# Experts' results weighted as they leave PSUM and summed by an adding scatter

## The chip, the cores and the metric

One core of a Trainium2 chip runs one program for the whole model: TensorE (PE) multiplies matrices, VectorE (DVE), ScalarE (ACT) and GpSimd (POOL) do the rest, SyncE (SP) issues most of the loads and stores, and 16 DMA engines move the data. The metric is the time of one execution on the device in microseconds, lower is better. All data are 32-bit.

## The reference

The model has two layers over 1024 tokens of width 1024 and 256 context tokens. Layer 0 mixes with differential attention, layer 1 with windowed attention. After each mixer stands a mixture of experts: a router picks one of 4 groups and in it 2 of 8 experts, so each token goes to 2 of 32 experts. The context tokens go through the experts in layer 0 alone, so layer 0 sends 1280 tokens and layer 1 sends 1024. Cut to what matters here:

```
weights = (gate_g * jax.nn.softmax(top_v, axis=-1)).reshape(-1)
expert = (g[:, None] * EXPERTS_PER_GROUP + top_i).reshape(-1)
...
hidden = jax.nn.silu(x_blk @ w_gate[e]) * (x_blk @ w_up[e])
return hidden @ w_down[e]
...
out = jnp.zeros((n_tok + 1, d), t.dtype).at[buf_tok].add(yb * buf_w[:, None].astype(yb.dtype))
```

The sum of a token's two weighted results is multiplied by a gate row and added to the residual stream. After layer 1 the sum is normalised and written out.

## The kernel before, in words

Tokens are handled in tiles of 128: ten in layer 0 (`NT`; tiles 8 and 9 are the context), eight in layer 1 (`NX`). A matrix is multiplied in two parts, a rounded one and the remainder, so every weight chunk is first split by ScalarE (`ehi`, L1154) and VectorE (`elo`, L1156).

The experts (`moe`, L1161) run in the order of a list. An expert has six weight chunks of 1 MB, four for gate and up, two for down. They come through a ring of 12 slots filled by SP's queue (`ring_load`, L1123); from chunk 160 of 192 on, only 7 slots are left. SP issues a load when the slot's last reader is done. GpSimd gathers an expert's token rows (`gather`, L1177) two experts ahead by the list `tI`. The down products stand in one PSUM tile `y`; `result` (L1225) copies its two halves to SBUF, and `scatter` (L1182) writes its rows to `ybs` in DRAM, one row for each pair of token and choice, at the places in `dI` (twice the token plus the choice). An expert has up to 128 rows; places beyond the count point outside the table, and nothing is moved for them. A loop for experts with more than 128 rows (`overflow`, L1332) follows.

The order of the experts' work on PE, ACT, DVE and POOL is written out by hand (`manual_schedule`). Elsewhere a scheduler sets the order of instructions on each queue when the program is built, SP's queue always.

Layer 1 begins with the first layer's sums: per tile two loads of 512 KB (`load_y`, L1394), one for each choice, then `combine` (L1412): ScalarE multiplies the first result by its weight, VectorE multiplies the second and adds, the gate row multiplies on VectorE or GpSimd, VectorE adds to the residual. `norm1_a` and `norm1_b` follow, and the attention's products.

The end (`final`, L1421) loads sixteen tiles, builds diagonal matrices of the weights (`dg`), and lets TensorE mix the two results of tiles 1 to 7 (`mix`, L1451); VectorE multiplies by the gate row (L1452), adds (L1457) and normalises (L1464).

## Time and profile before

| | |
|---|---|
| runs timed alone | 2995.53 us median of 3 (2992.17 to 2997.57) |
| profiled execution | 2986.94 us, span 2985.0 us |
| granted TensorE clock, mean | 0.97 |
| PE / DVE / ACT / POOL busy | 93% / 78% / 73% / 30% of the span |
| DMA | 746 MB, 250 GB/s over the span |

A row of a timeline gives start, length, engine, line, operation and what is written from what, and in brackets the idle time before it with what ended it. A row of stretches gives the busy time of each engine in the stretch, the granted clock as a share of full speed, the mean busy share of the 16 DMA engines (transfers that overlap can take it over 1) and the GB/s moved. A row of lines gives count, total busy time, mean length and idle time before. Times of one execution are compared with that execution alone; busy shares over the whole span mix stages with different limits, so the stage is looked at first.

### The profile page before, as it was taken

What the parts mean: (1) busy time and instruction counts of PE and PEld (TensorE: products, weight loads), DVE (VectorE), ACT (ScalarE), POOL (GpSimd) and SP (SyncE); (2) the same over time, 40 slices, a digit from 0 to 9 for tenths busy, and PEclk for the clock granted to TensorE, in tenths of its full rate; (3) what the DMA queues carried; (4) which work ended last, traced back from release to release, by engine and by line L of the source; (5) the groups of instructions that cost most, each with busy time, mean ns of one, the idle gap of its engine ahead of it and who ended that gap; (6) DMA issues with size and microseconds to landing.
All of it is one profiled execution on the core that took longest, in us unless ns stands there. A gap on an engine that the chain in (4) does not pass through costs nothing. (4 is left out here: it accounts for less than half of the span.)

```text
span 2985.0 us, 44431 instructions
## 1 busy us (share of the span) xinstructions
PE 2786.2 (93%) x15263; PEld 2357.7 (79%) x15263; DVE 2340.4 (78%) x4063; ACT 2165.9 (73%) x3972; POOL 896.6 (30%) x839
## 2 busy tenths in 40 slices
PE   7999999999979979999999589998999799999996
PEld 4888888889868868888888478887888688888883
DVE  5778777777777779899998786665766799999987
ACT  5777777777678568888888578876553488888883
POOL 5756665665500011111110344655100111111110
PEclk9999999999989989999999699999999899999998
DMA  7644554454343689999999745444226799999996
GB/s 269 228 166 165 174 184 154 164 175 150 121 156 124 213 304 379 385 384 384 381 359 351 287 159 196 162 150 156 94 102 209 256 365 377 378 380 373 348 378 256
DMA packets 303502, 746.04 MB, mean 250 GB/s; under 512 B 24644, under 2 KB 80552, under 8 KB 287912
## 3 DMA queue, kind: packets, MB, share of 16 engines
q1 hardware_dynamic: 265320, 681.25, 63.4%
q0 software_dynamic: 19584, 41.98, 3.6%
q10 hardware_dynamic: 18368, 19.93, 1.9%
q8 instruction: 122, 2.00, 0.3%
q14 instruction: 108, 0.88, 0.1%
HBM read 681.13 MB, written 91.29 MB: 259 GB/s over the span
## 5 line engine op out<-in xcount | busy, mean ns | idle before, releaser
L1156 DVE TENSOR_TENSOR elo<-wr,ehi 128x1024 fp32r<-128x1024 f32 x768 | 894.4, 1219 | 106.3 <-ACT ehi L1154 106.3
L1154 ACT ACTIVATE ehi<-wr 128x1024 fp32r<-128x1024 f32 x768 | 765.7, 1065 | 6.7 <-DVE wts L1018 3.4
L344 PE MATMUL qkv<-w_hi,hT 128*128 128x384 f32 (+1 forms) x1920 | 542.0, 350 | 11.6 <-ACT hT L315 3.6
L344 PEld LDWEIGHTS qkv<-w_hi,hT 128*128 128x128 f32 x1920 | 351.2, 195 | 27.0 <-issue 10.8
L1183 POOL DMA_INDIRECT y_s<-yb,dI x64 | 65.6, 1025 | 966.8 <-ACT yb L1232 938.0
L344 PE MATMUL qkv<-w_lo,hT 128*128 128x384 f32 (+1 forms) x960 | 333.3, 347 | 0.0
L1222 PE MATMUL y<-ehi,hidT 128*128 128x512 f32 x1024 | 317.2, 391 | 2.4 <-ACT yb L1232 2.4
L1208 PE MATMUL pg<-ehi,xT 128*128 128x512 f32 x1024 | 291.9, 407 | 0.0
L1208 PE MATMUL pu<-ehi,xT 128*128 128x512 f32 x1024 | 281.9, 397 | 0.0
L605 DVE TENSOR_SCALAR_CACHE_REDUCE E<-S 128x1280 f32<-128x1280 f32 (+1 forms) x160 | 203.5, 1272 | 58.5 <-PE S L622 55.5
L1222 PEld LDWEIGHTS y<-ehi,hidT 128*128 128x128 f32 x1024 | 191.7, 188 | 44.0 <-ACT yb L1232 3.2
L613 ACT ACTIVATE E<-E,mx 128x1280 f32<-128x1280 f32 (+1 forms) x160 | 190.9, 1193 | 48.1 <-DVE E L605 46.9
L1208 PEld LDWEIGHTS pu<-ehi,xT 128*128 128x128 f32 x1024 | 187.9, 188 | 36.8
L1208 PEld LDWEIGHTS pg<-ehi,xT 128*128 128x128 f32 x1024 | 184.6, 190 | 33.5 <-ACT xT L1193 0.5
L864 PE MATMUL qkv<-woh,oT 128*128 128x512 f32 x576 | 200.2, 408 | 0.5 <-ACT oT L851 0.5
L1222 PE MATMUL y<-elo,hidT 128*128 128x512 f32 x512 | 199.4, 389 | 0.0
L344 PEld LDWEIGHTS qkv<-w_lo,hT 128*128 128x128 f32 x960 | 186.4, 194 | 6.2 <-issue 4.3
L620 PE MATMUL S<-K,Qh 128*128 128x512 f32 (+1 forms) x416 | 153.7, 370 | 17.7 <-DVE E L605 17.6
L227 ACT ACTIVATE mpr<-mraw,sf 128x256 f32<-128x256 f32 x320 | 145.3, 504 | 26.9 <-POOL macc L230 22.2
L1208 PE MATMUL pg<-elo,xT 128*128 128x512 f32 x512 | 159.0, 392 | 0.0
L1232 ACT ACTIVATE yb<-y 128x512 f32<-128x512 f32 x126 | 68.6, 595 | 124.4 <-PE y L1222 124.4
L1208 PE MATMUL pu<-elo,xT 128*128 128x512 f32 x512 | 158.2, 390 | 0.0
(306 smaller groups left out, 6482.7 us busy)
## 6 DMA issues: line engine op xcount, KB each, us to landing
wr<-in_wg SPq DMA_DIRECT2D x128, 1024.0 KB
wr<-in_wu SPq DMA_DIRECT2D x128, 1024.0 KB
wr<-in_wd SPq DMA_DIRECT2D x128, 1024.0 KB
hT<-hTs SPq DMA_DIRECT2D x100, 1024.0 KB
mraw<-in_mod_w SPq DMA_DIRECT2D x80, 512.0 KB
hTs<-hT SPq DMA_DIRECT2D x20, 1024.0 KB
c_y<-y_s SPq DMA_DIRECT2D x36, 512.0 KB
w_raw<-in_a_qkv SPq DMA_DIRECT2D x32, 384.0 KB
```

The source lines that it names most:

```text
L227: nc.scalar.activation(pr[v][:, q], raw[:, q], AF.Copy, scale=self.sf[:, 4 * i + q, v:v + 1])
L344: self.nc.tensor.matmul(ps[:, 0:n], hT[:, a, k, :], W[b][:, k, c0:c0 + n], start=(i == 0), stop=(i == 3 * KC - 1))
L605: nc.vector.tensor_scalar(E[:, 0:n], Sf[:, 0:n], -0.125, None, op0=OP.mult, op1=OP.min, accum_out=mx)
L613: nc.scalar.activation(E[:, 0:n], E[:, 0:n], AF.Exp, bias=mx, scale=-1.0, accum_out=acc)
L620: nc.tensor.matmul(Sf[:, n0:n0 + w], Qh[:, m, j * P:(j + 1) * P], K[h][:, m, o:o + w], start=True, stop=False)
L864: nc.tensor.matmul(y, oT[:, a, k, :], w[:, k, half * 512:half * 512 + 512], start=(i == 0), stop=(i == 3 * KC - 1))
L1154: nc.scalar.activation(hi, raw, AF.Copy)
L1156: nc.vector.tensor_tensor(lo[:, 0:c], raw[:, 0:c], hi[:, 0:c].bitcast(F32), op=OP.subtract)
L1183: nc.gpsimd.indirect_dma_start(out=self.ybs[l], out_offset=bass.IndirectOffsetOnAxis(ap=idx, axis=0), in_=yb, in_offset=None, bounds_check ...
L1208: nc.tensor.matmul(o, xt[:, a, k, :], w[:, q * 512:(q + 1) * 512], start=(k == 0 and a == 0 and w is hi), stop=(k == KC - 1 and w is lo))
L1222: nc.tensor.matmul(y[:, half, :], hT[:, a, k, :], w[:, f], start=(k == 0 and a == 0 and w is hi), stop=(k == 3 and w is lo))
L1232: nc.scalar.activation(yb[:, f], y[:, half, :], AF.Copy)
```

## The change

The table `ybs` has one row per token instead of two. Its rows are set to zero by 18 stores of a small zero tile, issued in the loop of attention 0. The router's weights are also written to DRAM (`ws`), two per token. For each expert GpSimd sets a column `we` to zero and gathers into it the 128 weights of the expert's rows, by `dI`. `result` multiplies by this column as it copies from PSUM. `scatter` goes by `tI` and has `compute_op=OP.add`: the DMA adds to the row that lies there. A tile's sum is then one load of 512 KB; `combine` multiplies by the gate row and adds, and `final` has neither the diagonals nor the mixing matmuls.

```diff
@@ consts
-        self.ybs = [dr.tile([2 * (NT, NX)[l] * P, D], F32, name=f"y_s{l}") for l in range(2)]
+
+        self.ybs = [dr.tile([(NT, NX)[l] * P, D], F32, name=f"y_s{l}") for l in range(2)]
+        self.ws = [dr.tile([2 * (NT, NX)[l] * P, 1], F32, name=f"w_s{l}") for l in range(2)]
+        self.zero = c.tile([P, 128], F32, name="zero")
+        nc.vector.memset(self.zero, 0.0)
@@ attention0, in the loop over heads and tiles
+                zeros = [self.ybs[l][t * P:(t + 1) * P, :] for l in range(2) for t in range((NT, NX)[l])][10 * (h - 1):10 * h] if h else []
                 for u, j in enumerate(range(NT) if nxt else ORDER0):
+                    for z in zeros[u:u + 1]:
+                        nc.sync.dma_start(z.rearrange("p (a b) -> p a b", a=8), bc(self.zero, 8, 1))
@@ finish, the last step of the router
             nc.vector.tensor_tensor(self.wts[:, 0:T, 1], gr, er, op=OP.mult)
+            nc.sync.dma_start(self.ws[l].rearrange("(t p a) o -> p t (a o)", p=P, a=2), self.wts[:, 0:T, :])
@@ moe
+            def gather_w(idx):
+
+                w = pl.tile([P, 1], F32, name="we", bufs=4)
+                nc.gpsimd.memset(w, 0.0)
+                nc.gpsimd.indirect_dma_start(out=w, out_offset=None, in_=self.ws[l],
+                                             in_offset=bass.IndirectOffsetOnAxis(ap=idx, axis=0),
+                                             bounds_check=2 * T * P - 1, oob_is_err=False)
+                return w
+
             def scatter(yb, idx):
+
                 nc.gpsimd.indirect_dma_start(out=self.ybs[l], out_offset=bass.IndirectOffsetOnAxis(ap=idx, axis=0),
-                                             in_=yb, in_offset=None, bounds_check=2 * T * P - 1, oob_is_err=False)
+                                             in_=yb, in_offset=None, bounds_check=T * P - 1, oob_is_err=False,
+                                             compute_op=OP.add)
...
-            def result(y, last=False):
+            def result(y, w, last=False):
...
-                        nc.vector.tensor_copy(yb[:, f], y[:, half, :])
+                        nc.vector.tensor_scalar(yb[:, f], y[:, half, :], w, None, op0=OP.mult)
...
-                        nc.scalar.activation(yb[:, f], y[:, half, :], AF.Copy)
+                        nc.scalar.activation(yb[:, f], y[:, half, :], AF.Copy, scale=w)
...
-                    yb = result(ys.pop(e), e == NE - 1)
-                    at(m + DSCAT, scatter, yb, self.dI[:, e:e + 1])
+                    yb = result(ys.pop(e), we.pop(e), e == NE - 1)
+                    at(m + DSCAT, scatter, yb, self.tI[:, e:e + 1])
...
                             ps[e] = [ps_g.tile([P, 512], F32, name=x) for x in ("pg", "pu")]
+                            we[e] = gather_w(self.dI[:, e:e + 1])
@@ load_y, combine
-    def load_y(self, l, t, pl, n=3, queues=None):
-        nc = self.nc
-        yt = [pl.tile([P, D], F32, name=f"c_y{a}", tag="c_y", bufs=2 * n) for a in range(2)]
-        for a in range(2):
-            (queues or (nc.sync, nc.sync))[a].dma_start(
-                yt[a], self.ybs[l][2 * t * P:2 * (t + 1) * P, :].rearrange("(p a) d -> p a d", a=2)[:, a, :])
+    def load_y(self, l, t, pl, n=3):
+        yt = pl.tile([P, D], F32, name="c_y", bufs=n)
+        self.nc.sync.dma_start(yt, self.ybs[l][t * P:(t + 1) * P, :])
         return yt
...
-        return self.load_y(l, t, pl, n), self.load_x(l, t, pl, CXB)
...
-        nc.scalar.activation(yt[0], yt[0], AF.Copy, scale=self.wts[:, t, 0:1])
-        nc.vector.scalar_tensor_tensor(yt[0], yt[1], self.wts[:, t, 1:2], yt[0],
-                                       op0=OP.mult, op1=OP.add)
-        eng.tensor_tensor(yt[0], yt[0], g2, op=OP.mult)
-        return lambda: nc.vector.tensor_tensor(xt, xt, yt[0], op=OP.add)
+        return self.load_y(l, t, pl, n + 1), self.load_x(l, t, pl, CXB)
+
+    def combine(self, yt, xt, g2, eng):
+
+        eng.tensor_tensor(yt, yt, g2, op=OP.mult)
+        return lambda: self.nc.vector.tensor_tensor(xt, xt, yt, op=OP.add)
@@ final
-            for t in range(1, NX):
-                dg[t] = pl.tile([P, 2, P], F32, name="dg", bufs=NX - 1)
...
-            def mix(t):
...
-                            nc.tensor.matmul(p[:, half, :], dg[t][:, a], y[t][a][:, f], start=(a == 0), stop=(a == 1))
-                    nc.vector.tensor_tensor(y0, p.rearrange("p a b -> p (a b)"), g2, op=OP.mult)
...
+            def add(t):
+
+                nc.vector.tensor_tensor(y[t], y[t], g2, op=OP.mult)
+                nc.vector.tensor_tensor(x[t], x[t], y[t], op=OP.add)
```

The order of instructions that the two programs hold shows where the new instructions stand. The first place is GpSimd's queue in the experts of layer 0, from the gather for expert 4 on; before (`xg` are gathered token rows, `h_s` the tokens, `y_s` the table of results, `yb` a result in SBUF):

```order
L1178 DMA xg_12188<-h_s_93,tI 128x1024
L1183 DMA y_s_98<-yb,dI 2560x1024
L1178 DMA xg_12186<-h_s_93,tI 128x1024
L1183 DMA y_s_98<-yb,dI 2560x1024
L1178 DMA xg_12187<-h_s_93,tI 128x1024
L1183 DMA y_s_98<-yb,dI 2560x1024
```

and after:

```order
L1186 DMA xg_12211<-h_s_93,tI 128x1024
L1201 DMA y_s_98<-yb,tI 1280x1024
L1193 MEMSET we 128x1
L1194 DMA we<-w_s_100,dI 128x1
L1186 DMA xg_12209<-h_s_93,tI 128x1024
L1201 DMA y_s_98<-yb,tI 1280x1024
L1193 MEMSET we 128x1
L1194 DMA we<-w_s_100,dI 128x1
L1186 DMA xg_12210<-h_s_93,tI 128x1024
L1201 DMA y_s_98<-yb,tI 1280x1024
```

For each expert a zeroing and a gather of the weight column came in ahead of the gather of rows; the scatter goes by `tI` into a table of half as many rows.

The second place is SP's queue early in attention 0, while the tiles of the first head are projected (`hTs` and `hT` are normalised tiles stored and loaded, `w_raw` and `mraw` weights); before:

```order
L317 DMA hTs_89<-hT 128x2048
L317 DMA hTs_90<-hT 128x2048
L487 DMA hT<-hTs_82 128x2048
L317 DMA hTs_91<-hT 128x2048
L487 DMA hT<-hTs_83 128x2048
L215 DMA mraw<-in_mod_w 128x4x256 x2
L330 DMA w_raw<-in_a_qkv 128x768
L487 DMA hT<-hTs_84 128x2048
```

and after:

```order
L321 DMA hTs_88<-hT 128x2048
L334 DMA w_raw<-in_a_qkv 128x768 x2
L321 DMA hTs_89<-hT 128x2048
L663 DMA y_s_98<-zero 1024x1x128 x2
L321 DMA hTs_90<-hT 128x2048
L491 DMA hT<-hTs_82 128x2048
L321 DMA hTs_91<-hT 128x2048
L663 DMA y_s_98<-zero 1024x1x128 x2
L491 DMA hT<-hTs_83 128x2048
L219 DMA mraw<-in_mod_w 128x4x256 x2
L491 DMA hT<-hTs_84 128x2048
L334 DMA w_raw<-in_a_qkv 128x768
```

Some of the 18 zero stores now stand between the stores and loads of tiles, one to three at a time.

The third place is SP's queue at the start of layer 1 (`c_y` results, `g` gate rows, `c_x` residual); before:

```order
L1398 DMA c_y_17986<-y_s_98 128x1024
L1398 DMA c_y_17987<-y_s_98 128x1024
L734 DMA g_1_17990<-mod_s_100 128x1024
L1398 DMA c_y_17992<-y_s_98 128x1024
L1398 DMA c_y_17993<-y_s_98 128x1024
L1398 DMA c_y_17996<-y_s_98 128x1024
L1398 DMA c_y_17997<-y_s_98 128x1024
L734 DMA g_0_18000<-mod_s_100 128x1024
L378 DMA cos<-in_cos 128x512
```

and after:

```order
L1416 DMA c_y<-y_s_98 128x1024
L741 DMA g_1_18176<-mod_s_104 128x1024
L1416 DMA c_y<-y_s_98 128x1024 x2
L741 DMA g_0_18182<-mod_s_104 128x1024
L382 DMA cos<-in_cos 128x512
L383 DMA sin<-in_sin 128x512
L741 DMA sink<-in_b_sink 128x16
```

One load stands for two, and the gate rows and the rope tables move up behind fewer loads.

## Rows read from the trace of the kernel before

**Rows 1.** The page, parts 1 and 2: PE's total, then 40 slices in tenths.
```profile
PE 2786.2 (93%) x15263; PEld 2357.7 (79%) x15263; DVE 2340.4 (78%) x4063; ACT 2165.9 (73%) x3972; POOL 896.6 (30%) x839
...
PE   7999999999979979999999589998999799999996
...
DVE  5778777777777779899998786665766799999987
...
PEclk9999999999989989999999699999999899999998
DMA  7644554454343689999999745444226799999996
```

**Rows 2.** Stretches of 100 us in layer 0's and layer 1's experts.
```profile
core 0: us, PE busy (x) PEld busy (x) DVE busy (x) ACT busy (x) POOL busy (x), PEclk, DMA share, GB/s
...
1300.00:1400.00 100.00, 100.00 (x474) 82.55 (x473) 89.83 (x89) 82.36 (x101) 15.11 (x12) 1.00 1.02 386
...
2500.00:2600.00 100.00, 100.00 (x474) 82.51 (x473) 91.52 (x93) 83.51 (x103) 13.64 (x11) 1.00 1.02 377
```

**Rows 3.** Timeline: layer 0's first and thirty-first scatter on GpSimd.
```profile
1107.10 1.02 POOL L1183 DMA_INDIRECT y_s<-yb,dI  x1 [21.67 <-ACT yb L1232]
...
1642.02 0.98 POOL L1183 DMA_INDIRECT y_s<-yb,dI  x1 [16.32 <-ACT yb L1232]
```

**Rows 4.** Groups of lines: the split on ScalarE, and layer 1's weighting.
```profile
L1154 ACT ACTIVATE ehi<-wr 128x1024 fp32r<-128x1024 f32 x768 | 765.7, 1065 | 6.7 <-DVE wts L1018 3.4 <-PE y L1222 1.5 <-PE pg L1208 1.3
...
L1416 DVE SCALAR_TENSOR_TENSOR c_y<-c_y,wts,c_y 128x1024 f32<-128x1024 f32 x10 | 18.0, 1797 | 5.5 <-ACT c_y L1415 3.1 <-DMA c_y<-y_s 2.2
...
L1415 ACT ACTIVATE c_y<-c_y,wts 128x1024 f32<-128x1024 f32 x10 | 11.4, 1141 | 5.1 <-DMA c_y<-y_s 5.1
```

**Rows 5.** Short stretches: attention 0, layer 0's experts, layer 1's start, its experts, the end.
```profile
180.00:200.00 20.00, 19.49 (x127) 17.39 (x126) 15.17 (x32) 12.39 (x30) 8.13 (x10) 1.00 0.39 139
...
1530.00:1540.00 10.00, 10.00 (x47) 8.26 (x47) 8.31 (x9) 8.11 (x11) 2.51 (x2) 1.00 0.86 315
...
1710.00:1720.00 10.00, 7.18 (x36) 6.53 (x35) 9.29 (x21) 5.60 (x13) 6.11 (x7) 0.83 0.96 374
...
2820.00:2830.00 10.00, 10.00 (x49) 8.25 (x48) 10.00 (x11) 8.84 (x11) 1.50 (x1) 1.00 0.74 246
...
2950.00:2960.00 10.00, 10.00 (x24) 4.37 (x23) 8.81 (x13) 2.60 (x6) 0.00 (x0) 1.00 1.03 411
```

**Rows 6.** DMA queues: packets, MB, share of 16 engines; SP's queue is q1.
```profile
q1 hardware_dynamic: 265320, 681.25, 63.4%
q0 software_dynamic: 19584, 41.98, 3.6%
```

**Rows 7.** Timeline: the last ring loads on SP and the last chunk's first read.
```profile
2899.96 6.11 SPq L1133 DMA_DIRECT2D wr<-in_wd  x3
...
2921.45 1.06 ACT L1154 ACTIVATE ehi<-wr 128x1024 fp32r<-128x1024 f32 x1
```

**Rows 8.** Timeline: VectorE on the first tile of layer 1.
```profile
1661.20 1.28 DVE L1416 SCALAR_TENSOR_TENSOR c_y<-c_y,wts,c_y 128x1024 f32<-128x1024 f32 x1 [2.19 <-DMA c_y<-y_s]
...
1663.08 1.23 DVE L1418 TENSOR_TENSOR c_y<-c_y,g 128x1024 f32<-128x1024 f32 x1 [0.60 <-DMA g<-mod_s]
...
1670.84 0.75 DVE L294 TENSOR_SCALAR n_xn<-xg,rsq 128x1024 f32<-128x1024 f32 x1
```

**Rows 9.** Timeline: VectorE at the end, tiles 0, 1, 2 and the last.
```profile
2940.30 0.76 DVE L1454 TENSOR_SCALAR c_y<-c_y,wts 128x1024 f32<-128x1024 f32 x1 [0.95 <-DMA c_y<-y_s]
...
2949.55 1.23 DVE L1452 TENSOR_TENSOR c_y<-mix,wr 128x1024 f32<-128x1024 f32 x1 [4.08 <-PE mix L1451]
...
2952.98 1.23 DVE L1452 TENSOR_TENSOR c_y<-mix,wr 128x1024 f32<-128x1024 f32 x1 [0.95 <-PE mix L1451]
...
2979.99 1.28 DVE L1464 SCALAR_TENSOR_TENSOR c_y<-wr,rsq,wr 128x1024 f32<-128x1024 f32 x1
```

**Rows 10.** The scatters' table: time from issue to landing.
```profile
DMA to landing us min/median/max: 3.2/7.4/8.6
```

More of the change, by code (lines that the diff above doesn't have):

```diff
@@ L1229, in result @@
                     if last and half:
-                        nc.vector.tensor_copy(yb[:, f], y[:, half, :])
+                        nc.vector.tensor_scalar(yb[:, f], y[:, half, :], w, None, op0=OP.mult)
                     else:
-                        nc.scalar.activation(yb[:, f], y[:, half, :], AF.Copy)
+                        nc.scalar.activation(yb[:, f], y[:, half, :], AF.Copy, scale=w)
                 return yb
-            ops = dict(gather=gather, scatter=scatter, transposes=transposes, parts=parts, gate_up=gate_up,
+            ops = dict(gather=gather, gather_w=gather_w, scatter=scatter, transposes=transposes, parts=parts, gate_up=gate_up,
                        hidden=hidden, down=down, result=result, xT_open=xT_open, hid_open=hid_open)
@@ L1246, in at @@
                     later.setdefault(m, []).append((f, a))
-                xts, hids, ps, ys, hl = {}, {}, {}, {}, {}
+                xts, hids, ps, ys, hl, we = {}, {}, {}, {}, {}, {}
                 def xT_half(e, half, m):
@@ L1390, in overflow @@
                     ops["down"](hT, y, 2 * (c - 4) + s, *self.split(raw[:, s * 1024:(s + 1) * 1024], pl))
-            ops["scatter"](ops["result"](y), dI)
-    def load_y(self, l, t, pl, n=3, queues=None):
-        nc = self.nc
-        yt = [pl.tile([P, D], F32, name=f"c_y{a}", tag="c_y", bufs=2 * n) for a in range(2)]
-        for a in range(2):
-            (queues or (nc.sync, nc.sync))[a].dma_start(
-                yt[a], self.ybs[l][2 * t * P:2 * (t + 1) * P, :].rearrange("(p a) d -> p a d", a=2)[:, a, :])
+            ops["scatter"](ops["result"](y, ops["gather_w"](dI)), tI)
+    def load_y(self, l, t, pl, n=3):
+        yt = pl.tile([P, D], F32, name="c_y", bufs=n)
+        self.nc.sync.dma_start(yt, self.ybs[l][t * P:(t + 1) * P, :])
         return yt
@@ L1409, in combine_load @@
     def combine_load(self, l, t, pl, n=3):
-        return self.load_y(l, t, pl, n), self.load_x(l, t, pl, CXB)
-    def combine(self, l, t, yt, xt, g2, eng):
-        nc = self.nc
-        nc.scalar.activation(yt[0], yt[0], AF.Copy, scale=self.wts[:, t, 0:1])
-        nc.vector.scalar_tensor_tensor(yt[0], yt[1], self.wts[:, t, 1:2], yt[0],
-                                       op0=OP.mult, op1=OP.add)
-        eng.tensor_tensor(yt[0], yt[0], g2, op=OP.mult)
-        return lambda: nc.vector.tensor_tensor(xt, xt, yt[0], op=OP.add)
+        return self.load_y(l, t, pl, n + 1), self.load_x(l, t, pl, CXB)
+    def combine(self, yt, xt, g2, eng):
+        eng.tensor_tensor(yt, yt, g2, op=OP.mult)
+        return lambda: self.nc.vector.tensor_tensor(xt, xt, yt, op=OP.add)
     def final(self):
@@ L1427, in final @@
             pl = self.pool(es, "fin", side="right")
-            ps = self.pool(es, "finp", bufs=4, space=PSUM)
             x = [self.load_x(1, t, pl, NX) for t in range(NX)]
@@ L1431, in final @@
             es.enter_context(tc.manual_schedule(engines=MOE_ENG))
-            dg = {}
-            for t in range(1, NX):
-                dg[t] = pl.tile([P, 2, P], F32, name="dg", bufs=NX - 1)
-                for a in range(2):
-                    nc.vector.tensor_scalar(dg[t][:, a], self.ident, self.wts[:, t, a:a + 1], None, op0=OP.mult)
             ss = pl.tile([P, NX], F32, name="ss")
@@ L1441, in final @@
             todo = deque()
-            def mix(t):
-                xt, (y0, y1) = x[t], y[t]
-                if t in dg:
-                    p = ps.tile([P, 2, 512], F32, name="mix")
-                    for half in range(2):
-                        f = slice(half * 512, half * 512 + 512)
-                        for a in range(2):
-                            nc.tensor.matmul(p[:, half, :], dg[t][:, a], y[t][a][:, f], start=(a == 0), stop=(a == 1))
-                    nc.vector.tensor_tensor(y0, p.rearrange("p a b -> p (a b)"), g2, op=OP.mult)
-                else:
-                    nc.vector.tensor_scalar(y0, y0, self.wts[:, t, 0:1], None, op0=OP.mult)
-                    nc.vector.scalar_tensor_tensor(y0, y1, self.wts[:, t, 1:2], y0, op0=OP.mult, op1=OP.add)
-                    nc.vector.tensor_tensor(y0, y0, g2, op=OP.mult)
-                nc.vector.tensor_tensor(xt, xt, y0, op=OP.add)
+            def add(t):
+                nc.vector.tensor_tensor(y[t], y[t], g2, op=OP.mult)
+                nc.vector.tensor_tensor(x[t], x[t], y[t], op=OP.add)
                 if t in (2, 4, 6):
@@ L1460, in mix @@
                     todo.extend([(t - 2, r[:, 0:1]), (t - 1, r[:, 1:2])])
-                nc.scalar.activation(y1, xt, AF.Square, accum_out=ss[:, t:t + 1])
+                nc.scalar.activation(y[t], x[t], AF.Square, accum_out=ss[:, t:t + 1])
             def out(t, r):
-                nc.vector.scalar_tensor_tensor(y[t][0], x[t], r, fg, op0=OP.mult, op1=OP.mult)
-                nc.sync.dma_start(A["out"][0, t * P:(t + 1) * P, :], y[t][0])
+                nc.vector.scalar_tensor_tensor(y[t], x[t], r, fg, op0=OP.mult, op1=OP.mult)
+                nc.sync.dma_start(A["out"][0, t * P:(t + 1) * P, :], y[t])
             for t in range(NX):
-                mix(t)
+                add(t)
                 if todo:
@@ L1573, in tick @@
                     yt, xt = ld.pop(t3)
-                    add = self.combine(0, t3, yt, xt, g2[0 if t3 < NX else 1], nc.vector if i < 1 else nc.gpsimd)
+                    add = self.combine(yt, xt, g2[0 if t3 < NX else 1], nc.vector if i < 1 else nc.gpsimd)
                     xs[t3] = xt
```

## The prediction

> **What bounds the kernel now.** I read the slices of the page first, then the stretches of the two expert stages, then the groups of lines with what ended their idle time, the DMA queues, and last the order of time at the two places where the change takes work away.
>
> The slices show two blocks in which TensorE, VectorE and the DMA engines all stand at 9, slices 15 to 22 and 32 to 39 [rows 1]. These are the expert stages, some 580 us each. In a stretch of 100 us there TensorE is busy for all of it at the full clock, and the DMA engines are too: share 1.02, 386 GB/s in layer 0 and 377 in layer 1 [rows 2]. From the first scatter of layer 0 to the thirty-first there are 534.9 us, 17.83 us an expert [rows 3]. In that time an expert needs six weight chunks of 1024 KB (6.29 MB) and, since 1280 tokens go to two experts each and there are 32 experts, 80 rows of 4 KB gathered and 80 scattered (0.66 MB). That is 6.95 MB in 17.83 us, 390 GB/s, against 386 moved; in layer 1, with 64 rows, 382 against 377. So the DMA engines have no idle time and supply a little less than TensorE takes. TensorE sets the pace only because the ring of weight chunks starts the stage filled, twelve chunks ahead: ScalarE, which reads every chunk first, waited 6.7 us before it in the whole run and not once for a load [rows 4]. Whatever adds DMA work to an expert first eats this lead, and then TensorE waits for weights.
>
> **The change part by part.**
>
> The scatter becomes an add. The rows moved stay the same, 2560 in layer 0 and 2048 in layer 1, but each must now also be read where it lands. The trace of before has no such transfer. The nearest rows are transfers of 4-KB rows without an add: the final tile loads, 411 GB/s at share 1.03 [rows 5]. The lower end is nothing, if the read of the old row goes beside the write at no cost to the engine. The upper end is two more row times, as if the old row were fetched and the sum written in transfers of their own. I take one: an add scatter moves what a scatter moves, and reads as many rows as a gather does. One row time each is 10.49 MB / 411 GB/s = 25.5 us of all 16 engines in layer 0 and 8.39 MB / 411 = 20.4 in layer 1.
>
> The Trainium skill has a price for this that no run here shows: "Collectives: The Full Stack", section "The bandwidth ceiling: the fold count and why AG ≠ RS ≠ AR", says that an add in the DMA engine needs two source reads where a copy needs one, and that a reduce-scatter therefore ran at half the rate of an all-gather. By that rule the sum would come out with one extra row time, as the bounds' middle does.
>
> The weight gathers add 64 transfers of 128 four-byte pieces on GpSimd's queue, 9216 small packets with their completions. The software queue moved 41.98 MB in 19584 packets in 3.6% of 16 engines' span, 1719 us; its rows are 41.98 MB / 4096 = 10249, at 16 x 4096 / 411e3 = 0.159 us 1634 us, so the other 9335 packets took about 85 us, 9 ns each [rows 6]. At that price the gathers cost 9216 x 9 ns / 16 = 5.2 us, 2.6 a layer. The upper end is the mean packet of the hardware queue, 63.4% of 47760 us over 265320 packets = 114 ns [rows 6], 8192 x 114 / 16 = 58 us. I take 5.2: the size is that of the small packets. GpSimd itself has room: a scatter there takes 0.98 to 1.02 us to issue [rows 3], and three issues per expert stand against 17.83 us.
>
> The last two scatters of a layer come after its last weight load, so 30 of 32 count: (25.5 + 20.4 + 5.2) x 30/32 = 47.9 us of added DMA work while weights are due. Off this goes the lead that is left at a layer's end. Its last three loads were issued from 2899.96 to 2906.07, and the last chunk is first read at 2921.45 [rows 7]: 15.4 us, of which its own transfer takes 1.05 MB / 385 GB/s = 2.7. The lead is thus between 0 (the load queued all that time) and 12.7 us. Near the layer's end the DMA engines once had nothing to do, share 0.86 and 0.74 in ten us [rows 5], for want of a free slot, so it isn't 0; I take 6 a layer. TensorE then loses 47.9 - 12 = 36 us.
>
> The multiplication where results leave PSUM is the same instruction with a scale. With a scale from a column, 128x1024 took 1141 ns, without one 1065 [rows 4]: under 0.1 us more twice an expert, on ScalarE, which is 82 to 84% busy [rows 2]. I cost it at nothing; if that cover were gone it would be 64 x 0.15 = 10 us. The weight it waits for is fetched an expert and a half earlier. The store of the weights stands on SP's queue among the first ring loads and holds one of them back until the weights are computed; the eleven chunks ahead of it last 11/6 x 17.83 = 33 us, so nothing waits.
>
> The 18 zero fills write 9.4 MB in attention 0: 23 us of DMA at 411 GB/s, in a stage where the engines stand at share 0.39 in such a stretch [rows 5]. They go onto SP's queue within the first fifth of that stage, ahead of loads that TensorE takes one tile at a time. Ends 0 and 10 us; I take 2, the queue being idle for most of a tile.
>
> The start of layer 1 loses per tile one 512-KB load, one ScalarE multiply (1141 ns) and one VectorE multiply-add (mean 1797 ns): 18.0 us of VectorE over ten tiles [rows 4]. VectorE is 93% busy in a stretch of it [rows 5]. The chain of the first tile shows the least gain: its multiply-add ran from 1661.20 to 1662.48, the next step waited for the row g until 1663.08, and the normalised tile came at 1670.84 after a second tile's multiply-add and two loads more [rows 8]; without them it comes 3 us earlier. The most is the 18.0 us. I take 9, half, as the gaps of TensorE there are shared between VectorE, ScalarE and loads. What is late next is VectorE's other work on the tile.
>
> The end loses eight loads and the 56 matmuls that mixed two results. Tile 0 starts at 2940.30 as before, give or take the landing of the last scatter. VectorE waited for the matmuls until 2949.55 and 2952.98, and from tile 2's product at 2952.98 to its last product at 2979.99 it was nearly dense [rows 9]. Now tiles 0 and 1 need two products and sums of 1.23 us each, so tile 2 begins at 2940.3 + 4 x 1.23 = 2945.2 instead of 2952.98, 7.8 us earlier. The last scatter adds and lands perhaps 1 us later. I take 7.
>
> Sum: +36 +2 -9 -7 = +22 us on the profiled execution's 2986.94, 3009. The runs that were only timed have a median of 2995.53, 8.6 us above it; added there, +22 gives 3018.
>
> **The rivals.**
>
> *The add is free* (the read of the old row hides in the engine). For it: the engine already reads and writes at once in every transfer. Against: at share 1.02 nothing about an engine is known to be idle. Then only the weight gathers eat lead, 2.6 us a layer of about 6, TensorE never waits, and the gains stay: -9 -7 +0 to 2, 2980 to 2982. It decides wherever the add costs under 0.35 of a row time, since 45.9 x 0.35 x 30/32 + 4.9 - 12 = 8 us of waiting leaves a gain of 6. This is the case on the other side.
>
> *The add costs two more row times or more.* For it: read, sum and write of one row depend on each other, and each scatter must land before the next is issued (landing took 7.4 us at the median [rows 10]). Then (91.8 + 5.2) x 30/32 - 12 = 79 us of waiting and 2995.5 + 79 - 14 = 3060; more if the granted clock falls in the pauses.
>
> *The waits and gains meet* (the add at 0.35 to 0.6 of a row time): within 6 us of before.
>
> **How the numbers follow.** Forecast 0.50, its own range 3002 to 3033 (lead 0 to 12.7 a layer, start of layer 1 3 to 18). Free add 0.25, costly add 0.17, balance 0.08. A change of under 0.2%, 6 us, can't be told from none here. Faster is the free add, 0.25; same the balance, 0.08; slower the other two, 0.67. The range runs from 2976, which leaves the far end of the free case, to 3052, which leaves about two thirds of the costly one.
>
> **What would show each step.** In the groups of lines of after, ScalarE's split (line of `ehi`) must wait for the loads of `wr`, some tens of us, late in each layer and hardly at all in its first half; the scatters must be more than 17.83 us apart there; the share of the software queue must grow from 3.6% to about 5.3%. VectorE's first product of the end must follow tile 0's load and be dense from then on; the first transposes of layer 1 must come 3 us or more earlier after the last scatter. If ScalarE never waits for `wr`, the price of the add is wrong and the kernel is faster; if the waits begin in the first ten experts, the add costs more than one row time.

## The result, and the profile after

The changed kernel takes 3071.0 us (median of four runs, 3068.67 to 3072.80) against 2993.85 (2986.52 to 2997.57): 1.0265 times the time before, 95% interval 1.0251 to 1.0279. The forecast was slower, 3018 in a range of 2976 to 3052; the direction was right, the loss, 77 us between the medians, is three and a half times the 22 of the forecast, and the time lies above the range. The profiled executions differ by 85.7 us of span (2985.0 and 3070.7), some 8 more than the medians.

The span is best cut at ScalarE's reads of the weight chunks. First come the first and the last chunk of each layer in the timeline after (start, length, engine, line, operation):

```profile
1075.38 1.04 ACT L1162 ACTIVATE ehi<-wr 128x1024 fp32r<-128x1024 f32 x1
...
1689.11 1.07 ACT L1162 ACTIVATE ehi<-wr 128x1024 fp32r<-128x1024 f32 x1
...
2400.34 1.04 ACT L1162 ACTIVATE ehi<-wr 128x1024 fp32r<-128x1024 f32 x1
...
3010.44 1.06 ACT L1162 ACTIVATE ehi<-wr 128x1024 fp32r<-128x1024 f32 x1
```

In the kernel before the first three of these reads are

```profile
1059.57 1.04 ACT L1154 ACTIVATE ehi<-wr 128x1024 fp32r<-128x1024 f32 x1
...
1638.38 1.06 ACT L1154 ACTIVATE ehi<-wr 128x1024 fp32r<-128x1024 f32 x1
...
2341.22 1.04 ACT L1154 ACTIVATE ehi<-wr 128x1024 fp32r<-128x1024 f32 x1
```

and the last is at 2921.45 [rows 7]. That gives five stages. The table has them for every kernel that was timed with a comparison, in us of the profiled execution:

| kernel | to the first chunk | experts 0 | between | experts 1 | end | median of runs |
|---|---|---|---|---|---|---|
| before | 1059.6 | 578.8 | 702.8 | 580.2 | 63.6 | 2993.9 |
| changed | 1075.4 | 613.7 | 711.2 | 610.1 | 60.2 | 3071.0 |
| no add (e1) | 1073.8 | 584.5 | 711.1 | 585.5 | 55.9 | 3013.8 |
| no weight gathers (e2) | 1071.0 | 611.6 | 714.7 | 608.6 | 59.7 | 3065.8 |
| no add, no fills (e3) | 1058.5 | 586.0 | 710.1 | 586.3 | 56.5 | 2999.6 |
| two plain scatters (e5) | 1071.8 | 614.4 | 720.9 | 612.7 | 60.1 | 3074.3 |
| half rows (e6) | 1063.6 | 615.2 | 709.9 | 617.7 | 60.5 | 3068.8 |
| fills by ScalarE (e7) | 1072.7 | 612.8 | 715.1 | 610.1 | 60.2 | 3072.0 |
| rows spread (e8) | 1073.3 | 609.5 | 714.8 | 603.0 | 60.1 | 3064.6 |
| before, spread (e9) | 1061.0 | 579.4 | 703.5 | 579.7 | 63.1 | 2990.4 |
| products on VectorE (e10) | 1072.0 | 612.3 | 706.5 | 610.8 | 60.5 | 3065.3 |
| fills late (e13) | 1062.3 | 612.4 | 712.4 | 607.7 | 60.1 | 3059.2 |
| three mends (e16) | 1061.1 | 610.9 | 705.3 | 606.3 | 60.5 | 3046.7 |

So the 85.7 us are +15.8 before the experts, +34.9 and +29.9 in them, +8.4 between and -3.4 at the end. Two stages of expert work agree within 4 us between kernels in which the same changes bear on them; the stage between varies more (710 to 721 us in the changed kernels that leave its work alone), so a difference of 5 us there says little. The slices and queues of the page after answer to [rows 1] and [rows 6]:

```profile
PE   7899999999989979999999589998999799999992
...
DMA  7774554454333699999999735444236799999996
...
q1 hardware_dynamic: 283784, 681.27, 62.3%
q0 software_dynamic: 21632, 42.03, 5.3%
```

At this resolution the two pages look alike; nothing in the slices tells of 65 us. The share of the software queue went from 3.6% to 5.3%, as forecast for one more row time: 162.7 us of 16 engines' time against 107.5, 55 more, where the forecast had 25.5 + 20.4 + 5.2 = 51.1. The stretches of the expert stages answer to [rows 2]:

```profile
1200.00:1300.00 100.00, 100.00 (x471) 81.98 (x470) 89.07 (x90) 84.65 (x102) 23.73 (x24) 1.00 1.01 354
...
1500.00:1600.00 100.00, 93.90 (x425) 73.11 (x424) 82.52 (x83) 75.88 (x92) 20.67 (x23) 1.00 1.01 354
...
2500.00:2600.00 100.00, 100.00 (x469) 81.95 (x468) 89.07 (x88) 83.06 (x101) 23.73 (x24) 1.00 1.00 351
...
2800.00:2900.00 100.00, 94.80 (x434) 74.80 (x433) 83.61 (x83) 77.27 (x94) 20.86 (x21) 1.00 0.97 351
```

The DMA engines are as busy as before but move 351 to 354 GB/s instead of 377 to 386. TensorE is busy for 100% early in each stage and for 94 to 95% late in it. The group of lines shows what it waits for, through ScalarE:

```profile
L1162 ACT ACTIVATE ehi<-wr 128x1024 fp32r<-128x1024 f32 x768 | 776.2, 1062 | 160.1 <-DMA wr<-in_wd 99.0 <-PE y L1241 16.1 <-DMA wr<-in_wu 14.3
...
L1201 POOL DMA_INDIRECT y_s<-yb,tI x64 | 104.1, 1626 | 922.3 <-ACT yb L1251 908.5 <-issue 7.9 <-DVE yb L1249 5.8
...
L1251 ACT ACTIVATE yb<-y,we 128x512 f32<-128x512 f32 x126 | 79.4, 680 | 57.5 <-PE y L1241 57.5
```

The split waited 6.7 us in all and never for a load [rows 4]; now it waits 160.1, mostly for the loads `wr`. In layer 0 the first of these waits stands at chunk 88 of 192, in the fifteenth expert (in layer 1 at chunk 83, in the fourteenth):

```profile
1357.09 1.07 ACT L1162 ACTIVATE ehi<-wr 128x1024 fp32r<-128x1024 f32 x1 [0.71 <-DMA wr<-in_wg]
```

### The profile page after: what moved, and what is told of

Read it like the earlier page. It is cut to its first block, busy times and chain, and to the rows that moved or that the text cites. A ratio compares the mean times of both kernels' runs of the same rounds, so it can differ in the third digit from the quotient of the medians.

```text
span 3070.7 us, 44447 instructions
## 1 busy us (share of the span) xinstructions
PE 2793.3 (91%) x15207; PEld 2346.0 (76%) x15207; DVE 2338.0 (76%) x4038; ACT 2165.2 (71%) x3960; POOL 991.8 (32%) x967
## 3 DMA queue, kind: packets, MB, share of 16 engines
q0 software_dynamic: 21632, 42.03, 5.3%
## 5 line engine op out<-in xcount | busy, mean ns | idle before, releaser
L1162 ACT ACTIVATE ehi<-wr 128x1024 fp32r<-128x1024 f32 x768 | 776.2, 1062 | 160.1 <-DMA wr<-in_wd 99.0
L1201 POOL DMA_INDIRECT y_s<-yb,tI x64 | 104.1, 1626 | 922.3 <-ACT yb L1251 908.5
L348 PEld LDWEIGHTS qkv<-w_hi,hT 128*128 128x128 f32 x1920 | 353.6, 196 | 38.1 <-issue 17.3
L1241 PE MATMUL y<-elo,hidT 128*128 128x512 f32 x512 | 208.1, 406 | 26.1 <-DVE elo L1164 25.8
L372 POOL TENSOR_TENSOR rd<-rp_a,rp_u 128x256 f32<-128x256 f32 (+1 forms) x96 | 88.7, 924 | 199.8 <-DVE rp_u L367 107.6
```

Of the source, the lines that this page charges most:

```text
L348: self.nc.tensor.matmul(ps[:, 0:n], hT[:, a, k, :], W[b][:, k, c0:c0 + n], start=(i == 0), stop=(i == 3 * KC - 1))
L372: nc.gpsimd.tensor_tensor(rd[:, :, 0, :], av, uu, op=OP.add)
L1162: nc.scalar.activation(hi, raw, AF.Copy)
L1201: nc.gpsimd.indirect_dma_start(out=self.ybs[l], out_offset=bass.IndirectOffsetOnAxis(ap=idx, axis=0), in_=yb, in_offset=None, bounds_check ...
L1241: nc.tensor.matmul(y[:, half, :], hT[:, a, k, :], w[:, f], start=(k == 0 and a == 0 and w is hi), stop=(k == 3 and w is lo))
```

## The experiments

**What the add costs (e1, e2, e5, e6).** e1 takes the add away and nothing else:

```diff
-                in_=yb, in_offset=None, bounds_check=T * P - 1, oob_is_err=False, compute_op=OP.add)
+                in_=yb, in_offset=None, bounds_check=T * P - 1, oob_is_err=False)
```

> The changed kernel whose scatter overwrites instead of adding, so that one of a token's two results is left out of the sum; weights, zero fills and single loads stay. In the two profiles the time from the first read of a weight chunk to the last grew from 578.8 to 613.7 us in layer 0 and from 580.3 to 610.1 in layer 1, 64.7 us in all. Theory A (the add carries it): the two stages fall back to within 10 us of before together, 1160 to 1170, and the whole to 3008 to 3020. Theory B (the 64 gathers of weights, small packets and one more completion each, carry most of it): the stages stay at 1200 or more and the whole at 3048 or more. Either way the 15.8 us that the first stage lost before its experts stay.

3013.82 us, 1.0084 [1.0067, 1.0101] of before; the two stages 1170.0 us. Theory A holds, at the upper end of what it allowed. The group of lines has no wait for a load any more:

```profile
L1162 ACT ACTIVATE ehi<-wr 128x1024 fp32r<-128x1024 f32 x768 | 765.3, 1063 | 6.9 <-DVE wts L1025 3.4 <-PE y L1240 1.6
```

The add thus carries 1223.8 - 1170.0 = 53.8 us of the two stages. The other 1170.0 - 1159.0 = 11 belong to the rest of the change. e2 leaves out the gathers of weights:

```diff
-                nc.gpsimd.memset(w, 0.0)
-                nc.gpsimd.indirect_dma_start(out=w, ..., in_=self.ws[l], ...)
+                nc.gpsimd.memset(w, 1.0)
```

> The changed kernel without the 64 gathers of weights (the column is set to one, so the weighting is left out); the add stays. Theory A: the two expert stages fall from 1223.8 us by 5 to 12 (their 2.6 us of transfers a layer, and a start without them), the whole to 3058 to 3068. Theory B: they fall by 40 or more, the whole to under 3032.

3065.76 us, the stages 1220.2, 3.6 less. Against theory B: the gathers are cheap. (1.4 short of the least that was expected.) e5 puts a second plain scatter in the add's place:

```diff
-                in_=yb, ..., compute_op=OP.add)
+                in_=yb, ...)
+                nc.gpsimd.indirect_dma_start(out=self.ybx[l], ..., in_=yb, ...)
```

> The changed kernel with two overwriting scatters for each expert (the second into a spare table) in place of one adding scatter; one result is left out of the sum. It calibrates the add in row times. If an add costs one row time more than a plain scatter, as the length of its packets says (327 ns against 159), the two expert stages come to 1224 within 8 us and the whole to 3071 within 8. If it costs two row times, they are 30 to 45 us shorter, the whole 3026 to 3041; if half, they are 15 to 30 us longer.

3074.25 us, the stages 1227.1, within 3.3 of the changed kernel, and a like share of the software queue:

```profile
L1163 ACT ACTIVATE ehi<-wr 128x1024 fp32r<-128x1024 f32 x768 | 777.3, 1061 | 167.2 <-DMA wr<-in_wd 95.9 <-DMA wr<-in_wu 20.5 <-DMA wr<-in_wg 16.5
...
q0 software_dynamic: 30848, 60.91, 5.2%
```

An adding scatter costs what two plain scatters cost: the chosen size of the add, one row time, was right as a unit. The rule that the prediction quoted, from the Trainium skill's "Collectives: The Full Stack", section "The bandwidth ceiling: the fold count and why AG ≠ RS ≠ AR", that an add needs two source reads, agrees with this measurement. e6 sends each row as two adding scatters of half rows, into two tables:

```diff
-                nc.gpsimd.indirect_dma_start(out=self.ybs[l], ..., in_=yb, ..., compute_op=OP.add)
+                for a in range(2):
+                    nc.gpsimd.indirect_dma_start(out=self.ybs[l][a], ..., in_=yb[:, a * 512:(a + 1) * 512], ..., compute_op=OP.add)
```

> The changed kernel with two tables of half rows: each expert's result goes out as two adding scatters of 2-KB rows, and a tile's sum is loaded in two halves; the same bytes in twice the packets, and one more issue on GpSimd. If the add costs by its bytes (a second read), the two expert stages stay at 1224 to 1240 us and the whole at 3071 to 3090. If it costs a fixed turn for each packet (327 - 159 = 168 ns of a 4-KB packet), 25.5 + 20.4 us of engine time come on top and the stages go to 1265 or more, the whole to 3112 or more.

3068.76 us, the stages 1232.9, 9 more than the changed kernel with twice the adding packets. The add goes by its bytes, with a small price for each transfer or packet on top. That the whole came out shorter than the 3071 expected is the first stage's doing, of which more under the fills.

**What one row time costs there (e11, e12).** If the unit was right, its price in time wasn't. To read the pace of the loads without TensorE's, one of the three products of every expert matmul is left out:

```diff
-                    for a, w in ((0, hi), (1, hi), (0, lo)):
+                    for a, w in ((0, hi), (0, lo)):
```

> The kernel before with one of the three products of each expert matmul left out (the remainder of the tokens times the rounded weight), so that TensorE needs a third less and the loads set the pace. It measures the pace of the DMA engines with plain scatters. From the first read of weight chunk 96 to that of chunk 191 the kernel before takes 279.7 us in both layers, TensorE's pace. Theory L (the engines were slower than TensorE already, so the lead of the ring was spent and nothing was left to set against the add): 289 to 296 us in layer 0, 284 to 292 in layer 1. Rival M (the engines had room): under 279.7, down to VectorE's 16 us an expert, 255.

> The changed kernel with the same product left out. Theory L (its pace is the loads' alone): the same 306.4 and 304.5 us between chunks 96 and 191 as the changed kernel, within 2, and against the kernel before with that product left out 12 to 15 us more, the add and the gathers at one row time, 0.9 us an expert. If TensorE shared in the pace, it falls by 5 us or more.

The reads of chunks 96 and 191 in layer 0 and in layer 1, of the kernel before without that product:

```profile
1337.12 1.07 ACT L1154 ACTIVATE ehi<-wr 128x1024 fp32r<-128x1024 f32 x1
...
1622.87 1.06 ACT L1154 ACTIVATE ehi<-wr 128x1024 fp32r<-128x1024 f32 x1
...
2613.01 1.08 ACT L1154 ACTIVATE ehi<-wr 128x1024 fp32r<-128x1024 f32 x1
...
2898.36 1.06 ACT L1154 ACTIVATE ehi<-wr 128x1024 fp32r<-128x1024 f32 x1
```

and of the changed kernel without it:

```profile
1370.36 1.07 ACT L1162 ACTIVATE ehi<-wr 128x1024 fp32r<-128x1024 f32 x1
...
1675.66 1.06 ACT L1162 ACTIVATE ehi<-wr 128x1024 fp32r<-128x1024 f32 x1
...
2694.29 1.06 ACT L1162 ACTIVATE ehi<-wr 128x1024 fp32r<-128x1024 f32 x1
...
2999.45 1.06 ACT L1162 ACTIVATE ehi<-wr 128x1024 fp32r<-128x1024 f32 x1
```

These 95 chunks are 15.8 experts. Before: 285.8 and 285.4 us, 18.05 us an expert, where TensorE needs 279.7, 17.67. After: 305.3 and 305.2, 19.28 an expert, and the changed kernel with all its products 306.4 and 304.5. So theory L holds in direction: the loads alone set the late pace after, and they were slower than TensorE already before. In size it fell short at both: the pace before came 3 us under the 289 expected in layer 0, and the add with its gathers costs 19.5 and 19.8 us over 95 chunks, not 12 to 15. That is 1.23 and 1.25 us an expert, and it is the same in both layers, although layer 1 moves a fifth fewer rows. (Whole times of these two, one run each: 2965.63 and 3063.03 us.)

The stretches and queues between these reads tell where the 19.5 and 19.8 us go. The kernel before without that product, layer 0 and then layer 1:

```profile
1337.12:1622.87 285.75, 237.56 (x941) 167.83 (x940) 255.96 (x252) 232.25 (x283) 35.31 (x29) 0.92 1.01 383
...
q1 hardware_dynamic: 41274, 99.53, 92.6%
q0 software_dynamic: 4176, 9.64, 8.6%
...
2613.01:2898.36 285.35, 236.41 (x942) 163.54 (x941) 256.44 (x252) 232.10 (x283) 35.56 (x29) 0.93 1.01 378
...
q1 hardware_dynamic: 41324, 99.89, 93.3%
q0 software_dynamic: 4176, 7.74, 7.1%
```

and the changed kernel without it:

```profile
1370.36:1675.66 305.30, 250.00 (x941) 179.15 (x940) 256.06 (x252) 234.66 (x283) 57.48 (x59) 0.86 1.00 358
...
q1 hardware_dynamic: 41281, 99.57, 87.4%
q0 software_dynamic: 4656, 9.65, 12.6%
...
2694.29:2999.45 305.16, 247.08 (x936) 173.59 (x935) 256.30 (x252) 234.62 (x283) 57.27 (x59) 0.88 0.99 354
...
q1 hardware_dynamic: 41347, 99.98, 88.3%
q0 software_dynamic: 4656, 7.75, 10.3%
```

The software queue's packets take 8.6% of 285.75, 24.6 us of 16 engines, and then 12.6% of 305.30, 38.5: 13.9 more in layer 0, and by the same sum 11.2 more in layer 1. The forecast's own prices give (25.5 + 2.6) x 95/192 = 13.9 and (20.4 + 2.6) x 95/192 = 11.4 for these 95 chunks. So the added DMA work was priced right; the loads lost 5.6 and 8.6 us more than this work. Of that, 2.2 and 3.2 us are the loads' own packets (q1), which took longer for the same bytes, and 3.4 and 5.4 stand in the lower mean share of the engines, 1.00 and 0.99 instead of 1.01.

**Do the rows lie on few engines? (e8, e9, e14, e15)** That would make the price alike in both layers. The routing of the reference gives 58 to 96 rows an expert in layer 0 and 39 to 104 in layer 1, always at the head of the 128 places. Which engine a place goes to, no trace here shows; the test takes eight neighbouring places to share one. The edit compares the rank with a permuted row of numbers:

```diff
-            nc.vector.tensor_tensor(oh, bc(self.iota, 2, 1), bc(self.r_all[:, tok(t), :], P, 2), op=OP.is_equal)
+            for a in range(2):
+                nc.vector.tensor_scalar(oh[:, a, :].rearrange("p (b c) -> p b c", b=16), self.iota.rearrange("p (c b) -> p b c", b=16),
+                                        self.r_all[:, tok(t), a:a + 1], None, op0=OP.is_equal)
```

> The changed kernel complete, but an expert's rows stand otherwise in the 128 places: row r goes to place (r mod 16)*8 + r/16 instead of place r. Theory C (the fullest engine sets the price): a transfer of 128 rows gives each of the 16 DMA engines eight neighbouring places, and since an expert has 80 or 64 rows on average, all at the head, the first engines carry eight of them each time, 256 a layer by the reference's routing, where the mean is 160 and 128. An added row time then costs 256 x 0.159 = 41 us a layer on the engine that ends last and not 25.5 and 20.4, which would explain why the whole price is 57 us. Spread, the fullest engine has 174 and 141 rows, 40 and 56 us less work over its gathers and adds; the two expert stages fall from 1223.8 us to 1159 to 1175 and the whole to 3008 to 3022. Theory D (the mean over the engines counts and the rest is a price of the add itself): the stages stay within 6 us of 1224, the whole within 6 of 3071. If neighbouring places went to different engines, the spread would make it slower.

> The kernel before with the same spread of rows. TensorE never waits for a load there, so both theories expect the expert stages to stay at 1159 us within 2 and the whole within 6 us of the kernel before. If the stages get shorter, something else than TensorE bounded them.

e8: 3064.57 us, the stages 1212.5: 11 less, not 50 to 65. e9: 2990.43 us, 1.0006 [0.9996, 1.0017], its stages as before, as both theories had it. The pace alone:

> The kernel before with one of three products left out and the rows of an expert spread over the 128 places. Theory C (few engines carry the rows): from chunk 96 to 191 less than the 285.8 and 285.4 us of the unspread one, by the rows that the fullest engine loses: 8 - 5.4 rows in layer 0 and 8 - 4.4 in layer 1, twice 0.159 us each, 13 and 18 us, so about 273 and 267, with layer 1 shorter. Theory D (not so): 285 within 3 in both.

> The changed kernel with the same product left out and the rows spread. Theory C: the add costs 0.8 and 0.65 us an expert against the spread kernel without it, 12 to 15 us in layer 0 and 10 to 13 in layer 1 over 95 chunks. Theory D: again 18 to 21 in both.

Spread, 95 chunks take 283.6 and 283.9 us without the add and 304.1 and 301.3 with it: 20.5 and 17.3 more. (Whole: 2957.00 and 3056.15 us, one run each.) Theory C falls as the main cause: without the add, spreading gave 2 us where 13 to 18 were expected, and the add costs as much as before in layer 0. Only in layer 1 does the add's price fall, from 19.8 to 17.3.

**The fills (e3, e7, e13).** e3 is e1 without the 18 stores:

```diff
-                    for z in zeros[u:u + 1]:
-                        nc.sync.dma_start(z.rearrange("p (a b) -> p a b", a=8), bc(self.zero, 8, 1))
```

> The overwriting kernel of this series (one result left out of the sum) without the 18 zero fills. Theory A (the fills and the loads that they push back on SP's queue cost attention 0 its 15.8 us): 12 to 16 us less than the overwriting kernel with fills, 2994 to 3006. Rival: the order of the first stage came out otherwise for other reasons (the weights' store, another pool), and the difference is under 4 us.

2999.55 us, the first chunk at 1058.5 instead of 1073.8: the fills cost 15 us, nearly all that the first stage lost. e7 issues them from ScalarE (`nc.scalar.dma_start`):

> The changed kernel with the 18 zero fills issued from ScalarE's queue in place of SP's; the same bytes at about the same time. Theory E (the fills cost by their place on SP's queue, behind which the weights and tiles of the first head wait): the first expert chunk is read 10 to 16 us earlier than at 1075.4, the whole 3055 to 3061. Rival F (they cost by the 9.4 MB that the DMA engines move in small pieces while tiles are loaded): within 5 us of 1075.4 and of 3071.

3071.99 us, the first chunk at 1072.7. It gave nothing back, but it doesn't refute the queue's place: ScalarE issued the fills between 1.1 and 106.4 us, where SP had done it between 52.9 and 194.6, so the time of the fills changed too. e13 holds them back, by making the zero tile from a tile that is loaded in the fifth step of the loop:

```diff
-        nc.vector.memset(self.zero, 0.0)
...
-                zeros = [...][10 * (h - 1):10 * h] if h else []
+                zeros = [...][10 * (h - 5):10 * (h - 4)] if h > 4 else []
+                if h == 5:
+                    nc.vector.tensor_scalar(self.zero, hTl[0][:, 0, 0, :], 0.0, None, op0=OP.mult)
```

> The changed kernel with the 18 zero fills held back to the sixth and seventh head of attention 0, where the DMA engines stand at share 0.45 and the weights of the first heads are long there; SP issues them. Theory F (the fills cost while the engines are at share 0.7 to 0.8 in the first 200 us): the first expert chunk is read at 1060 to 1066 instead of 1075.4, the whole 3056 to 3062. Rival N (23 us of writes cost the same wherever a tile's load stands behind them): 1071 to 1077, the whole 3066 to 3076.

```profile
L664 SPq DMA_DIRECT2D y_s<-zero x18: 518/668/6896, 615.3 to 679.3; - x18
```

3059.17 us, the first chunk at 1062.3: 13 of the 15.8 us are back with the same stores from the same queue. So the fills don't cost by their bytes. Nor does the time at which they go out decide alone: in e6 they go out between 53.9 and 193.3 us, from the same queue, as 36 stores of half the size, and the first chunk is read at 1063.6, 11.8 us earlier than in the changed kernel. Whether it was the transfers, or what SP's queue had in which order, is not told apart.

**The start of layer 1 (e10).**

```diff
-                    add = self.combine(yt, xt, g2[...], nc.vector if i < 1 else nc.gpsimd)
+                    add = self.combine(yt, xt, g2[...], nc.vector)
```

> The changed kernel with all gate-row products at the start of layer 1 on VectorE, where six are on GpSimd. In the profile after, VectorE's adds there take 2.20 us where they took 1.22, and single small steps up to 6 us, beside GpSimd's products of 2.4 us. Theory G (GpSimd's products, which now start at once, stretch VectorE's work and eat the gain): from the last chunk read of layer 0 to the first of layer 1 it takes 700 to 706 us instead of 711.2, the whole 3060 to 3066. Rival H (VectorE is simply the bound there): 6 x 1.22 = 7 us more of it, 711 to 719, the whole 3071 to 3079.

3065.28 us; the stage between takes 706.5 instead of 711.2. VectorE's adds in the changed kernel, and in e10:

```profile
L1432 DVE TENSOR_TENSOR c_x<-c_x,c_y 128x1024 f32<-128x1024 f32 x7 | 15.4, 2202 | 1.1 <-DMA c_x<-x_s 1.1
```

```profile
L1432 DVE TENSOR_TENSOR c_x<-c_x,c_y 128x1024 f32<-128x1024 f32 x7 | 9.0, 1287 | 1.2 <-DMA c_x<-x_s 1.2
```

Theory H is out, and theory G's range is missed by half a microsecond: taking GpSimd's products away makes the adds 0.9 us shorter each, and the stage 4.7 us, though VectorE now has six products more. That is little more than this stage varies, but e16 repeats it (705.3). A second cause goes away with the same edit: on GpSimd's own queue the products stand between the steps that write `hT`, and TensorE waits for these,

```profile
L348 PE MATMUL qkv<-w_hi,hT 128*128 128x384 f32 (+1 forms) x208 | 65.2, 383 | 11.3 <-POOL hT L320 6.8 <-ACT hT L319 4.1 <-DMA hT<-hTs 0.3
```

6.8 us in the changed kernel against 1.6 before and 2.8 in e10. So e10 speaks for GpSimd's products costing the stage something, and doesn't tell whether by slowing VectorE or by delaying `hT`. The other 3.7 us of the 8.4 stay unexplained.

**Together (e16).** Spread, late fills and VectorE's products in one kernel:

> The changed kernel complete, with rows spread, zero fills held back to the sixth and seventh head, and all gate-row products on VectorE. If the three causes are apart, their gains add up: 1223.8 - 1212.5 = 11 us of the expert stages, 13 before them, 5 between them, together 29 off 3071: 3038 to 3046. It stays slower than before either way, since the add's bytes stay. If it is over 3052, they share a cause.

3046.68 us (3041.65 to 3051.42), 1.0182 [1.0161, 1.0203]: 24 us back, against 29 in sum. The fills and products kept their gains (1061.1 and 705.3); of the spread's 11 us only 6.6 came. With the add, no version came near the kernel before, and without it (e3) the rest of the change still stood at 1.0036 [1.0021, 1.0050]; no version that keeps the whole computation as it is and beats both came out of this.

## Why the prediction was wrong

**What held.** The mechanism and its place: the expert stages, through the ring and ScalarE's split, from about the middle of each layer. The unit of the add, one more row time, by e5 and by the queue's 5.3%. The gathers of weights were cheap, 5.2 us forecast and 3.6 measured, though that was partly luck: the software queue has 2048 packets more (21632 against 19584), not 9216. The rival of a free add is refuted by e1, that of two row times by e5.

**The step that failed most: from added DMA work to time lost, "TensorE then loses 47.9 - 12 = 36 us".** The work itself, (25.5 + 20.4 + 5.2) x 30/32 = 47.9 us, came out as priced: over 95 chunks its packets took 13.9 and 11.2 us where 13.9 and 11.4 were forecast. The prediction then let the loads lose just this time. Measured as pace (e12 against e11), they lose 39.3 us over 190 chunks, so 79 over the 384 of both layers and 74 by the same 30/32: one and a half times the work. The lead set against it was underrated, not overrated: 74 - 53.8 = 20 us where 12 were taken. It is used up in the fourteenth or fifteenth expert, since the loads, already 0.38 us an expert slower than TensorE, are now 1.6 slower. The prediction's own sign of a dearer add, waits in the first ten experts, stayed away because the larger lead hid it. The error in the loads' loss, +26, outweighs that of the lead, -8; what is left of the two stages' loss, 11 us, is the next point but one.

Why a scatter of 64 rows holds the loads back as long as one of 80 (1.25 and 1.23 us, where bytes at 411 GB/s give 0.64 and 0.80) stays open, beyond the two parts named above: longer packets of the loads and a lower share of the engines. It is not a property of adding, since a plain second scatter costs the same (e5). Few engines explain little of it (e14, e15). The number of packets and transfers is little of it, since twice the adding packets cost 9 us (e6).

**"I cost it at nothing" (weighting at PSUM).** The copy out of PSUM rose from a mean of 595 ns to 680 (the line of `yb` above), 0.17 us an expert on ScalarE.

```profile
L1232 ACT ACTIVATE yb<-y 128x512 f32<-128x512 f32 x126 | 68.6, 595 | 124.4 <-PE y L1222 124.4
```

Nothing shows that this cost time, and the place of the loss speaks against it. e1 has the stages 11 us longer than before with no wait for loads, and no term of the sum had them. Some 5 of these lie in the first 24 chunks of the two layers (88.0 and 88.9 us against 85.4 and 86.8): TensorE waits 12.9 and 13.5 us for the first gathered rows, where it waited 9.9 and 11.0. Without the gathers of weights it still waits 14.4 and 12.2 (e2; 15.2 and 13.3 in the changed kernel), so these are about 1 us of it. The other 6 are spread evenly, 281.4 us instead of 279.7 from chunk 96 to 191, and lie in the down products, of which each takes 4 to 5 ns longer, without a wait. Between these reads in layer 0, before and then e1:

```profile
L1222 PE MATMUL y<-ehi,hidT 128*128 128x512 f32 x250 | 77.4, 391 | 0.0
L1222 PE MATMUL y<-elo,hidT 128*128 128x512 f32 x125 | 48.7, 389 | 0.0
...
L1240 PE MATMUL y<-ehi,hidT 128*128 128x512 f32 x250 | 78.6, 395 | 0.0
L1240 PE MATMUL y<-elo,hidT 128*128 128x512 f32 x125 | 49.3, 394 | 0.0
```

Why they are slower is open.

**The fills, "I take 2".** They cost 15 (e3). The bound of 10 was read from the share of 0.39 in the stretch of 180 to 200 us [rows 5]. The fills went out from 52.9 to 194.6 us, 14 of 18 before that stretch. But a higher share there doesn't explain the cost: 13 of them went out after 140 us, and the kernel before has

```profile
150.00:175.00 25.00, 24.59 (x146) 21.61 (x145) 19.26 (x36) 19.06 (x44) 13.31 (x16) 0.95 0.49 169
...
600.00:700.00 100.00, 95.49 (x617) 87.15 (x617) 75.05 (x149) 75.17 (x170) 62.80 (x60) 1.00 0.48 165
```

a like share where e13's fills went out, which cost 2.7. What failed is the step from a free share to a free store; which order on SP's queue makes it dear stays open (e6).

**The start of layer 1, "I take 9".** It became 8.4 slower. The first multiply with the gate row came no earlier, since the row `g` was late, as it stood 0.6 us behind before [rows 8]:

```profile
1713.70 1.23 DVE L1431 TENSOR_TENSOR c_y<-c_y,g 128x1024 f32<-128x1024 f32 x1 [5.79 <-DMA g<-mod_s]
...
1736.44 5.44 DVE L1432 TENSOR_TENSOR c_x<-c_x,c_y 128x1024 f32<-128x1024 f32 x1
```

The first transpose on TensorE came 24.5 us after the last expert matmul, before 24.1. Then GpSimd's products, freed of what they had waited for, ran in a burst beside VectorE's adds (1.22 us before, 2.20 after; one took 5.44). The Trainium skill, "Trainium Architecture — The Big Picture", section "What this means for kernel authors", says that VectorE and GpSimd share a pair of ports under an exclusive lock; the trace agrees: in the 5.44 us of that add GpSimd was busy from 1735.99 to 1740.79, and in e10, without the products, the adds take 1.29. Of the 18.0 us taken off VectorE, 6.9 went into these seven adds (15.4 us against 8.5) and 5.3 into two small steps of the norm, while other steps gave back some 2.5. How much of the stage's 8.4 us this is, e10 can't say, as it also takes the products out of the way of `hT`.

**The end, "I take 7".** It gave 3.4. The products do run densely: from the first to the last it takes 31.7 us instead of 39.7 [rows 9].

```profile
3033.81 1.23 DVE L1450 TENSOR_TENSOR c_y<-c_y,wr 128x1024 f32<-128x1024 f32 x1 [13.29 <-DMA c_y<-y_s]
...
3065.55 1.28 DVE L1458 SCALAR_TENSOR_TENSOR c_y<-wr,rsq,wr 128x1024 f32<-128x1024 f32 x1
```

But the first one comes 23.4 us after the last chunk read, not 18.9: the adding scatter at the end cost 4.5, not 1. With a plain one (e1) the first product comes 19.0 us after that read, and the end takes 55.9, 7.7 less than before, so the 7 was right but for the add.

The range ended at 3052 because the costly add was given 0.17. Its bounds asked how long the added packets take, and that was right; what a stream that fills the engines loses beside them, no row of the kernel before could show, and that needed a wider end. Summed up by stage, the forecast missed by 29 us in the experts, 14 before them, 17 between them and 4 at the end, all to the same side, so that no stage made up for another.

## What to carry to other kernels

Where DMA engines and TensorE both stand at 100%, ask which of the two is slower and is living on a lead: leave out some of TensorE's work, and the pace of the loads shows. Price an added transfer in such a stage by that pace, with and without it, and not by the time of its own packets: here the loads lost one and a half times that. And a step taken off an engine is a gain only if what it frees doesn't run into the next step: here longer steps beside GpSimd's freed products took back about half of VectorE's saving.

## What was not expected of the hardware

- An adding scatter lands later and keeps GpSimd longer: from issue to landing 9.2 us at the median against 7.4 [rows 10], and 1.63 us of GpSimd's time against 1.02 (1.02 for the plain scatter of e1 too).

```profile
DMA to landing us min/median/max: 6.1/9.2/10.4
```

- The add, with the gather of weights, costs saturated loads 1.2 us an expert, with 80 rows and with 64, though its packets take 0.88 and 0.71.
- The lightened kernel before is 25 us faster in its one run though its loads are slower than TensorE was. It gains while the lead lasts, 17 us in the first 96 chunks of each layer, and loses 6 after them.
